# Decoder layer on one core: reordered projections and a batched block-inverse merge

## Chip, cores and metric

The kernel runs on one core of a Trainium2 chip. The metric is the device time of one execution in microseconds (us), and the figure that counts is the median of the runs of a kernel. The core has four compute engines with a queue of their own each: PE (TensorE: matrix products into PSUM; its weight loads are shown apart as PEld), DVE (VectorE), ACT (ScalarE) and POOL (GpSimd). SP (SyncE) issues most of the transfers, ACT the others. Each engine works through its queue in the order in which the program left it.

## What is computed

One layer of a hybrid decoder on x of 1024 tokens by 1024 features, in float32. Cut to what matters here:

```python
h = rmsnorm(x, attn_norm_w)
proj = h @ w_in                       # 1024 x 3592
qkv_la, z_la, b_la, a_la, q_d, k_d, v_d = split(proj)
# group 1: gated DeltaNet, 4 heads of 128
q_la, k_la, v_la = split(silu(causal_conv(qkv_la, conv_w)))
L   = where(strict, (k_beta @ k^T) * decay, 0);  A = L + I     # per chunk
u, w = solve_lower_triangular(A, [v*beta, k_beta*exp(g)])
o_la = recurrence over the chunks with state S (128 x 128 per head)
o_la = rmsnorm(o_la, la_norm_w) * silu(z_la)
# group 2: differential attention, 4 heads, two softmax maps of 64 columns each
p   = softmax(q0 k0^T + bias) - lam * softmax(q1 k1^T + bias)
o_d = rmsnorm(p @ v_d) * (1 - lam_init)
x = x + concat([o_la, o_d]) @ w_out
x = x + (silu(h2 @ gate) * (h2 @ up)) @ w_down                 # h2 = rmsnorm(x)
return rmsnorm(x, final_norm_w)
```

The reference solves chunks of 64 tokens; the kernel uses chunks of 128, 8 per head, 32 in all.

## The kernel before

Every large product is split into three: an operand is a high part (`_h`) and a low part (`_l`, the rest), and `mm3` issues high x high, high x low and low x high into the same PSUM tile (L144, L145, L146). A projection of 128 output columns over all 1024 tokens, called a dense here, is 2 halves x 8 blocks of the input features x 3, so 48 products of 128x128 by 512 into one `big` tile of PSUM (128x1024). There are two `big` tiles, and four of 128x512 (`sm` and `fl`, two each), which the function `sm()` hands out in turn. A dense needs its 128 columns of weights in SBUF (`w_raw`, loaded by SP), their high part (`w_h`, ACT, L151) and their low part (`w_l`, on DVE in one instruction, L153, or on POOL in two, L157; an argument chooses).

The stages around the change, in the order of time:

- Conv, K and Q of the four DeltaNet heads (`dense_T` and `conv_silu`: ACT L433 and L437, three times DVE L435), the sums of squares, and the products K K^T and K Q^T (L478, L479), from which `At` and `intra` are made on DVE (L482, L485).
- The inverse of the 32x32 blocks on the diagonals, on DVE alone: four transposes (L504), then 31 times a product (L509) and a subtraction (L511), each in need of the one ahead, then two transposes (L514, L515) that give `DcT` and `Dc`. Beside it PE computes the four Z projections (`dense_T` with POOL for the low part, `silu` on ACT, a write to DRAM) and the V projection of head 0.
- Merging the 32-blocks to the inverse of 128x128 (`TT`), head by head: DVE spreads `DcT` and `Dc` to 128 columns (L537), then two levels of `At` x columns (L544, copied out by ACT L547), the upper update (L551) and in level 0 the lower one (L557), in two halves of four chunks, each product 128x128 by 128 though only some of the columns are read (L560, L563, L566). That is 40 products per head, 160 in all. A float32 product stands in the trace as two entries of PE, so a group of four is shown as x8.
- Transposes of K (L575) and V (L625), V projections of heads 1 to 3, the recurrence over 8 chunks (L640 to L680), and beside and behind the recurrence the attention's query and key projections of heads 0 and 1 (`qk_dense`): ACT L596 scales a half out of PSUM, ACT L597 rounds it to the high part, POOL L598 subtracts, and ACT issues the writes of `qh`, `ql` and `ks` to DRAM.
- Attention. SP loads `aqh`, `aql` (L720), `ak` (L702), `bias` (L705) and `avd` (L727) of head 0 from DRAM, and the first score product is L904. The order from here on is written out by hand, with projections of heads 2 and 3 as filler.

A scheduler that places each instruction orders the queues of PE, DVE, ACT, POOL and SP ahead of the attention, so code order and queue order differ.

Of the kernel before, what the change touches and what calls it, by code (L numbers as in the profile page):

```python
# [68 lines left out]
def decoder_kernel(ctx: ExitStack, tc: tile.TileContext, a: dict, out: bass.AP):  # L69
# [425 lines left out]
    def bx(name):  # L495
        return op.tile([P, T], F32, name="av", bufs=4)
# [16 lines left out]
    Dc = bx("Dc").rearrange("p (h c) -> p h c", c=32)  # L513
    nc.vector.transpose(out=DcT.rearrange("p h c -> p c h"), in_=X)  # L514
    nc.vector.transpose(out=Dc.rearrange("p h s -> p s h"), in_=X.rearrange("p c s -> p s c"))  # L515
    for h in range(H):
        zps = dense_T(C_Z + h * P, nc.gpsimd)
        sz = cvt()
        nc.scalar.activation(out=sz, in_=zps, func=AF.Silu)
        nc.scalar.dma_start(out=sz_dr[h], in_=sz)  # L520

    vts = []

    def v_dense(h):
        vt = cvt()
        conv_silu(dense_T(C_V + h * P, nc.gpsimd), 8 + h, vt)
        vts.append(vt)

    v_dense(0)
    TT = [opt("avl") for h in range(H)]  # L530
    quad_b = quad.rearrange("p (o q c) -> p o q c", o=1, q=4).broadcast_to([P, 8, 4, 32])
    K = []
    for h in range(H):
        Df = bx("Df").rearrange("p (j c) -> p j c", c=P)
        for dst, src in ((TT[h], DcT), (Df, Dc)):
            sb = src[:, h * 8:h * 8 + 8, :].rearrange("p j (o c) -> p j o c", o=1).broadcast_to([P, 8, 4, 32])
            nc.vector.tensor_tensor(out=dst.rearrange("p j (q c) -> p j q c", q=4), in0=sb, in1=quad_b, op=ALU.mult)  # L537
        Z1 = bx("Z1").rearrange("p (j c) -> p j c", c=P)
        for level in range(2):
            for half in range(2):  # L540
                b0 = h * 8 + half * 4
                ps = sm()
                for jj in range(4):
                    nc.tensor.matmul(ps[:, jj * P:(jj + 1) * P], lhsT=At[:, b0 + jj, :], rhs=Df[:, half * 4 + jj, :],  # L544
                                     start=True, stop=True)
                zs = Z1[:, half * 4:half * 4 + 4, :]
                nc.scalar.copy(out=zs, in_=ps.rearrange("p (a b) -> p a b", a=4))  # L547
                ut = sm()
                utv = ut.rearrange("p (a b) -> p a b", a=4)
                for jj in range(4):  # L550
                    nc.tensor.matmul(ut[:, jj * P:(jj + 1) * P], lhsT=Z1[:, half * 4 + jj, :], rhs=TT[h][:, half * 4 + jj, :],  # L551
                                     start=True, stop=True)
                if level == 0:
                    un = sm()
                    unv = un.rearrange("p (a b) -> p a b", a=4)
                    for jj in range(4):
                        nc.tensor.matmul(un[:, jj * P:(jj + 1) * P], lhsT=TT[h][:, half * 4 + jj, :], rhs=Z1[:, half * 4 + jj, :],  # L557
                                         start=True, stop=True)
                    for r0 in (0, 64):
                        nc.vector.tensor_scalar(out=TT[h][r0:r0 + 32, half * 4:half * 4 + 4, r0 + 32:r0 + 64],  # L560
                                                in0=utv[r0:r0 + 32, :, r0 + 32:r0 + 64],
                                                scalar1=-1.0, scalar2=None, op0=ALU.mult)
                        nc.scalar.mul(out=Df[r0 + 32:r0 + 64, half * 4:half * 4 + 4, r0:r0 + 32],  # L563
                                      in_=unv[r0 + 32:r0 + 64, :, r0:r0 + 32], mul=-1.0)
                else:
                    nc.vector.tensor_scalar(out=TT[h][0:64, half * 4:half * 4 + 4, 64:128], in0=utv[0:64, :, 64:128],  # L566
                                            scalar1=-1.0, scalar2=None, op0=ALU.mult)
    Ktok = gp.tile([P, NHJ, P], F32, name="ak", bufs=1)
    for h in range(H):
        Kh = Ktok[:, h * 8:h * 8 + 8, :]  # L570
        for half in range(2):
            ps = sm()
            for jj in range(4):
                j = half * 4 + jj
                nc.tensor.transpose(ps[:, jj * P:(jj + 1) * P], KT[h][:, j * P:(j + 1) * P], ident)  # L575
            nc.scalar.copy(out=Kh[:, half * 4:half * 4 + 4, :], in_=ps.rearrange("p (a b) -> p a b", a=4))
        K.append(Kh)


    def qk_dense(h, is_q, ps_of, mid=None):  # L580
        if (h, is_q) not in raws:
            fetch((h, is_q), *qk_col(h, is_q))
        w = take((h, is_q), nc.gpsimd if h > 1 else None)
        yield 0
        sh = cvt(F32R)
        sl = cvt(F32R)
        for n in range(2):
            if n and mid:
                mid()
            ps = ps_of(n)  # L590
            wh, wl = w
            ns = slice(n * 512, (n + 1) * 512)
            for k in range(NK):
                mm3(ps, wh[:, k, :], wl[:, k, :], xT_h[:, k, ns], xT_l[:, k, ns], k == 0, k == NK - 1)
                yield 3
            nc.scalar.mul(out=sl[:, ns].bitcast(F32), in_=ps, mul=DH ** -0.5 if is_q else 1.0)  # L596
            nc.scalar.copy(out=sh[:, ns], in_=sl[:, ns].bitcast(F32))  # L597
            nc.gpsimd.tensor_tensor(out=sl[:, ns], in0=sl[:, ns].bitcast(F32), in1=sh[:, ns].bitcast(F32),  # L598
                                    op=ALU.subtract)
        if is_q:  # L600
            nc.scalar.dma_start(out=qh_dr[h], in_=sh.bitcast(F32))
# [9 lines left out]
    def run(gen):  # L611
        for _ in gen:
            pass

    Vn = [opt("av") for h in range(H)]
# [794 lines left out]
```

## Time and profile before

| | us |
|---|---|
| median of 3 runs | 1379.53 (1378.08 to 1379.64) |
| profiled execution | 1377.38 |
| its span in the trace | 1375.5 |
| PE busy | 1305.1 (95% of the span) |
| DVE busy | 768.1 (56%) |
| ACT busy | 497.1 (36%) |
| POOL busy | 262.5 (19%) |

The mean granted clock of TensorE over the span is 0.988 of full speed. An idle row of the timeline carries in brackets how long its engine stood before it and what released it. All moments below are us from the start of the span.

### The profile page before, as it was taken

How to read it: one execution, taken by the hardware profiler on the slowest of the kernel's cores; microseconds unless marked ns; L12 is line 12 of the kernel's file. 1: busy time of each engine (PE TensorE's matmuls, PEld its weight loads, DVE VectorE, ACT ScalarE, POOL GpSimd, SP SyncE). 2: the span in 40 equal slices, each digit the busy share in tenths (PEclk: the TensorE clock that was granted, in tenths of full speed). 3: DMA queues.
4: the chain of work that ended last, by engine and by line, in shares of the span. 5: the costliest groups of instructions: out<-in, count | busy, mean ns of one | idle time of the engine just before them, and what ended most of it. 6: DMA issues, size and time to landing. Idle time of an engine off the chain costs nothing.

```text
span 1375.5 us, 17042 instructions
## 1 busy us (share of the span) xinstructions
PE 1305.1 (95%) x6540; PEld 1086.2 (79%) x6540; DVE 768.1 (56%) x1282; ACT 497.1 (36%) x948; POOL 262.5 (19%) x211
## 2 busy tenths in 40 slices
PE   6999999899988998998889999999999999999997
PEld 6968888798967777887667877787878788788886
DVE  6516649625833675876884555455545536545325
ACT  5233321233733654553543333232323235112104
POOL 1010052100042331113332121211121214200003
PEclk9999999999998999999999999999999999999999
DMA  7321113101055655734432233222222248422003
GB/s 216 110 62 47 31 44 97 29 1 47 1 145 182 208 179 185 237 119 168 145 100 77 94 100 98 79 75 92 92 77 73 80 134 280 152 92 92 0 1 123
DMA packets 122425, 143.31 MB, mean 104 GB/s; under 512 B 13632, under 2 KB 90728, under 8 KB 122344
## 3 DMA queue, kind: packets, MB, share of 16 engines
q1 hardware_dynamic: 114432, 128.07, 30.0%
q10 hardware_dynamic: 7912, 14.16, 2.8%
q8 instruction: 51, 0.84, 0.3%
q14 instruction: 30, 0.25, 0.1%
HBM read 103.40 MB, written 38.80 MB: 103 GB/s over the span
## 4 chain that ended last, share of the span: by engine, by line
PE 70%; DVE 13%; DMA 5%; issue 4%; ACT 4%; POOL 3%; SPq 1%; POOLq 0%; DVEq 0%; ACTq 0%
PE big L1177 17%; PE sm L1177 8%; PE fl L144 4%; PE fl L145 4%; PE fl L146 4%; PE fl L1177 4%; PE big L144 3%; PE big L145 3%; PE big L146 3%; PE sm L144 3%; PE sm L146 3%; PE sm L145 3%; PE sm L961 1%; DVE tmp L509 1%; DMA ks<-cv 1%
## 5 line engine op out<-in xcount | busy, mean ns | idle before, releaser
L144 PE MATMUL big<-xT_h,w_h 128*128 128x512 f32 x320 | 127.8, 399 | 0.7 <-DVE cv L435 0.7
L146 PE MATMUL big<-xT_h,w_l 128*128 128x512 f32 x320 | 126.9, 397 | 0.5 <-DVE w_l L153 0.5
L145 PE MATMUL big<-xT_l,w_h 128*128 128x512 f32 x320 | 126.2, 394 | 0.0
L1190 DVE TENSOR_TENSOR av<-big,av 128x512 f32<-128x512 f32 x88 | 60.5, 689 | 109.3 <-PE big L1177 109.2
L157 POOL TENSOR_TENSOR w_l<-w_raw,w_h 128x512 fp32r<-128x512 f32 x36 | 49.0, 1384 | 244.0 <-ACT w_h L151 244.0
L1177 PE MATMUL big<-hT_h,cv 128*128 128x512 f32 x264 | 90.8, 405 | 2.4 <-DVE av L1190 2.4
L1177 PE MATMUL big<-hT_h,avl 128*128 128x512 f32 x264 | 89.2, 399 | 1.1 <-DVE av L1190 1.1
L151 ACT CAST w_h<-w_raw 128x1024 fp32r<-128x1024 f32 x32 | 33.5, 1051 | 110.5 <-PE big L145 94.7
L144 PEld LDWEIGHTS big<-xT_h,w_h 128*128 128x128 f32 x320 | 60.7, 190 | 13.9 <-issue 2.2
L146 PEld LDWEIGHTS big<-xT_h,w_l 128*128 128x128 f32 x320 | 60.5, 189 | 13.2 <-DVE w_l L153 0.9
L145 PEld LDWEIGHTS big<-xT_l,w_h 128*128 128x128 f32 x320 | 60.6, 189 | 12.1 <-issue 0.2
L1177 PEld LDWEIGHTS big<-hT_h,cv 128*128 128x128 f32 x264 | 50.4, 191 | 20.2 <-DVE av L1190 9.8
L1177 PEld LDWEIGHTS big<-hT_h,avl 128*128 128x128 f32 x264 | 49.5, 188 | 18.1 <-DVE av L1190 8.0
L1177 PE MATMUL sm<-hB_h,avl 128*128 128x512 f32 x176 | 58.8, 395 | 1.1 <-ACT hB_h L1107 1.1
L1082 POOL TENSOR_TENSOR avl<-xh,avl 128x512 fp32r<-128x512 f32 x23 | 30.8, 1338 | 148.2 <-ACT avl L1081 148.2
L1190 DVE TENSOR_TENSOR x<-fl,x 128x512 f32<-128x512 f32 x48 | 33.0, 687 | 45.6 <-PE fl L146 45.6
L1190 DVE TENSOR_TENSOR x<-sm,x 128x512 f32<-128x512 f32 x48 | 33.0, 687 | 44.8 <-PE sm L146 44.1
L1177 PE MATMUL sm<-hB_h,cv 128*128 128x512 f32 x176 | 57.9, 389 | 0.0
L919 ACT ACTIVATE ae<-big,mx 128x128 f32<-128x128 f32 (+7 forms) x64 | 47.3, 741 | 27.7 <-DVE mx L910 11.6
L1082 POOL TENSOR_TENSOR cv<-xh,cv 128x512 fp32r<-128x512 f32 x22 | 28.3, 1288 | 146.3 <-ACT cv L1081 146.3
L1145 DVE TENSOR_TENSOR xh<-w_raw 128x512 f32<-128x512 f32 x45 | 31.0, 689 | 45.1 <-DMA w_raw<-in_w_gate_up 45.1
L435 DVE SCALAR_TENSOR_TENSOR cv<-big,convw,cv 128x1023 f32<-128x1023 f32 (+2 forms) x36 | 46.0, 1278 | 15.0 <-ACT cv L433 14.4
(431 smaller groups left out, 3532.1 us busy)
## 6 DMA issues: line engine op xcount, KB each, us to landing
w_raw<-in_w_gate_up SPq DMA_DIRECT2D x44, 512.0 KB, 4.0
w_raw<-in_w_in SPq DMA_DIRECT2D x24, 512.0 KB, 4.0
act<-av SPq DMA_DIRECT2D x22, 512.0 KB, 2.6
w_raw<-act SPq DMA_DIRECT2D x22, 512.0 KB, 4.2
cv<-in_w_down SPq DMA_DIRECT2D x20, 512.0 KB, 4.4
xt<-in_x SPq DMA_DIRECT2D x8, 512.0 KB, 5.5
ks<-cv ACTq DMA_DIRECT2D x8, 512.0 KB, 12.5
aqh<-qh SPq DMA_DIRECT2D x16, 256.0 KB, 5.2
```

Source lines behind the costliest of these rows:

```text
L144: nc.tensor.matmul(ps, lhsT=lh, rhs=rh, start=start, stop=False)
L145: nc.tensor.matmul(ps, lhsT=lh, rhs=rl, start=False, stop=False)
L146: nc.tensor.matmul(ps, lhsT=ll, rhs=rh, start=False, stop=stop)
L151: nc.scalar.copy(out=h, in_=raw)
L157: eng.tensor_tensor(out=l[:, c], in0=raw[:, c], in1=h[:, c].bitcast(F32), op=ALU.subtract)
L435: nc.vector.scalar_tensor_tensor(out=acc[:, d:], in0=ps[:, :T - d], scalar=convw[:, ct, 3 - d:4 - d], in1=acc[:, d:], op0=ALU.mult, op1=AL ...
L509: nc.vector.tensor_tensor(out=tv, in0=B[:, i + 1:, i:i + 1].broadcast_to([P, nr, ncol]), in1=X[:, i:i + 1, :ncol].broadcast_to([P, nr, nco ...
L919: nc.scalar.activation(out=e[:, :n].rearrange("p (b c) -> p b c", b=nb), in_=s[:, :, :w], func=AF.Exp, bias=mx[:, m:m + 1], accum_out=zs[: ...
L1082: eng.tensor_tensor(out=l, in0=raw, in1=h.bitcast(F32), op=ALU.subtract)
L1145: nc.vector.tensor_tensor(out=r, in0=a0, in1=a1, op=alu)
L1177: nc.tensor.matmul(ps, lhsT=x[:, k, :], rhs=y[:, k, :], start=begin and k == 0 and n == 0, stop=k == HALF - 1 and n == 2, skip_group_check ...
L1190: nc.vector.tensor_tensor(out=out, in0=in0, in1=in1, op=ALU.add)
```

## The change

- The Z projections leave the place beside the inverse. They come behind the recurrence, with their low weight parts on DVE.
- The query and key projections of attention heads 0 and 1 (four `qk_dense`) take their place beside the inverse. For these two heads ACT writes the scaled half as the high part, and one DVE instruction (L536 of the new file) reads the same half from PSUM and gives the low part; POOL has no part in it.
- V of heads 0 and 1 are both computed ahead of the merging.
- The merging goes level by level over the four heads, with eight chunks in one PSUM tile. `sub_z` (L594) takes 64 columns of the moving operand, `un` (L606) 32, and both `ut` (L608, L621) have 64 columns in the stationary operand and 64 in the moving one. The number of products stays 160. The spreads (L583) write 64 columns of `Dc` in place of 128.

The diff, cut to its core (the lines of the new file are 21 to 23 higher from the attention on):

```diff
-    for h in range(H):
-        zps = dense_T(C_Z + h * P, nc.gpsimd)
-        ...
-    v_dense(0)
+    for h in range(2):
+        run(qk_dense(h, True, wide()))
+        run(qk_dense(h, False, wide()))
...
+    v_dense(0)
+    v_dense(1)
...
-            nc.scalar.mul(out=sl[:, ns].bitcast(F32), in_=ps, mul=DH ** -0.5 if is_q else 1.0)
+            scale = DH ** -0.5 if is_q else 1.0
+            if h < 2:
+                nc.scalar.mul(out=sh[:, ns], in_=ps, mul=scale)
+                nc.vector.scalar_tensor_tensor(out=sl[:, ns], in0=ps, scalar=scale, in1=sh[:, ns].bitcast(F32),
+                                               op0=ALU.mult, op1=ALU.subtract)
+                continue
+            nc.scalar.mul(out=sl[:, ns].bitcast(F32), in_=ps, mul=scale)
             nc.scalar.copy(out=sh[:, ns], in_=sl[:, ns].bitcast(F32))
             nc.gpsimd.tensor_tensor(out=sl[:, ns], in0=sl[:, ns].bitcast(F32), in1=sh[:, ns].bitcast(F32),
...
+    def sub_z(h):
+        ps = sm()
+        for j in range(NT):
+            nc.tensor.matmul(ps[:, j * 64:(j + 1) * 64], lhsT=At[:, h * 8 + j, :], rhs=cols[h][:, j, :],
+                             start=True, stop=True)
+        nc.scalar.copy(out=Z1[h], in_=ps.rearrange("p (j c) -> p j c", c=64))
...
+        for j in range(NT):
+            nc.tensor.matmul(un[:, j * 32:(j + 1) * 32], lhsT=TT[h][:, j, :], rhs=Z1[h][:, j, 0:32], start=True, stop=True)
+        for j in range(NT):
+            nc.tensor.matmul(ut[0:64, j * 64:(j + 1) * 64], lhsT=Z1[h][:, j, :], rhs=tth[:, j, :, 32:64],
+                             start=True, stop=True)
...
-        if h > 0:
+        if h > 1:
             v_dense(h)
...
-    for h in range(2):
-        run(qk_dense(h, True, wide()))
-        run(qk_dense(h, False, wide()))
+    for h in range(H):
+        zps = dense_T(C_Z + h * P, nc.vector)
+        sz = cvt()
+        nc.scalar.activation(out=sz, in_=zps, func=AF.Silu)
+        nc.scalar.dma_start(out=sz_dr[h], in_=sz)
```

On the queue of DVE at the start of the inverse there stood, before (`av` holds the blocks and their inverse, `ak` is `At`):

```order
L504 STREAM_TRANSPOSE av<-ak 32x1024 x4
L509 TENSOR_TENSOR tmp<-av 128x31
L511 TENSOR_TENSOR av<-av,tmp 128x31
L509 TENSOR_TENSOR tmp<-av 128x60
L511 TENSOR_TENSOR av<-av,tmp 128x30x2
L509 TENSOR_TENSOR tmp<-av 128x87
L511 TENSOR_TENSOR av<-av,tmp 128x29x3
```

and now, with `cv<-big,cv` the new evacuation of a query or key half:

```order
L504 STREAM_TRANSPOSE av<-ak 32x1024 x4
L536 SCALAR_TENSOR_TENSOR cv<-big,cv 128x512
L509 TENSOR_TENSOR tmp<-av 128x31
L153 TENSOR_TENSOR w_l<-w_raw,w_h 128x1024
L511 TENSOR_TENSOR av<-av,tmp 128x31
L509 TENSOR_TENSOR tmp<-av 128x60
L511 TENSOR_TENSOR av<-av,tmp 128x30x2
L509 TENSOR_TENSOR tmp<-av 128x87
```

Between the transposes and L514 there are now five L536 and two L153, one more L536 stands behind L515 and one behind the spreads. The eighth, of the first half, stands ahead of the transposes.

On the queue of PE at the same place, the change from the second dense of that stretch to the third read, before (`big_1805` and `big_1864` are Z of heads 1 and 2):

```order
L145 MATMUL big_1805<-xT_l_138,w_h_1800 128x512
L146 MATMUL big_1805<-xT_h_137,w_l_1801 128x512
L144 MATMUL big_1864<-xT_h_137,w_h_1859 128x512 [waits Activation_49]
L145 MATMUL big_1864<-xT_l_138,w_h_1859 128x512
L146 MATMUL big_1864<-xT_h_137,w_l_1860 128x512 [waits Pool_49]
L144 MATMUL big_1864<-xT_h_137,w_h_1859 128x512
```

and now (`big_1739` and `big_1802` are query and key of head 0, `big_1865` the query of head 1):

```order
L145 MATMUL big_1802<-xT_l_138,w_h_1805 128x512
L146 MATMUL big_1802<-xT_h_137,w_l_1806 128x512
L144 MATMUL big_1865<-xT_h_137,w_h_1868 128x512 [waits DVE_49]
L145 MATMUL big_1865<-xT_l_138,w_h_1868 128x512
L146 MATMUL big_1865<-xT_h_137,w_l_1869 128x512 [waits DVE_49]
L144 MATMUL big_1865<-xT_h_137,w_h_1868 128x512
L145 MATMUL big_1865<-xT_l_138,w_h_1868 128x512
L146 MATMUL big_1865<-xT_h_137,w_l_1869 128x512
L144 MATMUL big_1865<-xT_h_137,w_h_1868 128x512
L144 MATMUL big_1802<-xT_h_137,w_h_1805 128x512 [waits DVE_49]
```

The tile that `big_1865` takes is that of `big_1739`, and the wait is now for DVE's L536 on it, where it was for ACT alone.

On the queue of PE at the entry to the attention there stood, before (`big_3344` is the key projection of head 1, `fl_3457` the filler):

```order
L145 MATMUL big_3344<-xT_l_138,w_h_3347 128x512
L146 MATMUL big_3344<-xT_h_137,w_l_3348 128x512
L144 MATMUL fl_3457<-xT_h_137,w_h_3450 128x512 [waits Activation_49]
L904 MATMUL big_3433<-ak_3425,aqh_3419 128x128 [waits DMAHW5_49,DMAHW6_49,DMAHW1_49,Activation_49]
L905 MATMUL big_3433<-ak_3425,aql_3422 128x128 [waits DMAHW7_49,DMAHW0_49]
```

and now (`big_3293` is Z of head 3):

```order
L145 MATMUL big_3293<-xT_l_138,w_h_3289 128x512
L146 MATMUL big_3293<-xT_h_137,w_l_3290 128x512
L927 MATMUL big_3369<-ak_3361,aqh_3355 128x128 [waits DMAHW3_49,DMAHW7_49,DMAHW0_49,Activation_49]
L928 MATMUL big_3369<-ak_3361,aql_3358 128x128 [waits DMAHW2_49,DMAHW1_49]
```

The score product waits for the same loads as before, but what stands ahead of it on PE is Z, 128 of whose 192 products are still to come when the recurrence ends. SP still issues the loads of the weights of the head 2 projections ahead of `aqh`.

## Rows read from the trace of the kernel before

**Rows 1.** Windows of 10 us; columns as the first line says, PEclk the granted clock.

```profile
core 0: us, PE busy (x) PEld busy (x) DVE busy (x) ACT busy (x) POOL busy (x), PEclk, DMA share, GB/s
...
240.00:250.00 10.00, 6.08 (x27) 4.69 (x25) 9.52 (x18) 2.06 (x2) 2.94 (x2) 1.00 0.19 52
250.00:260.00 10.00, 8.32 (x42) 7.55 (x43) 9.93 (x9) 1.43 (x4) 0.55 (x1) 0.66 0.22 53
...
410.00:420.00 10.00, 2.76 (x9) 2.40 (x10) 0.57 (x2) 1.21 (x2) 1.26 (x1) 0.54 0.98 322
```

**Rows 2.** PE's timeline at the merging: start, duration, line, operation [idle before, releaser].

```profile
239.80 0.39 PE L144 MATMUL big<-xT_h,w_h 128*128 128x512 f32 x1
...
245.69 0.39 PE L146 MATMUL big<-xT_h,w_l 128*128 128x512 f32 x1
251.68 2.08 PE L544 MATMUL fl<-av,ak 128*128 128x128 f32 x8 [5.60 <-DVE av L537]
...
253.98 0.63 PE L145 MATMUL big<-xT_l,w_h 128*128 128x512 f32 x1
...
256.12 0.63 PE L144 MATMUL big<-xT_h,w_h 128*128 128x512 f32 x1
...
257.71 1.06 PE L557 MATMUL fl<-av,avl 128*128 128x128 f32 x8
258.60 1.06 PE L544 MATMUL sm<-av,ak 128*128 128x128 f32 x8
```

**Rows 3.** PE's timeline at the first score product.

```profile
417.24 0.45 PE L904 MATMUL big<-ak,aqh 128*128 128x128 f32 x1 [10.43 <-DMA ak<-ks]
...
418.66 0.63 PE L146 MATMUL fl<-xT_h,w_l 128*128 128x512 f32 x1
...
420.37 0.63 PE L144 MATMUL big<-xT_h,w_h 128*128 128x512 f32 x1
```

**Rows 4.** The chain that ended last, ahead of that product: start, duration, what.

```profile
392.87 1.83 POOL cv L598
...
394.73 13.25 DMA ks<-cv
...
408.04 9.11 DMA ak<-ks
```

**Rows 5.** DVE's timeline over the inverse.

```profile
207.67 8.13 DVE L504 STREAM_TRANSPOSE av<-ak 32x1024 f32<-32x1024 f32 x4
215.83 1.20 DVE L509 TENSOR_TENSOR tmp<-av 128x31 f32<-128x31 f32 x1
...
225.36 1.52 DVE L509 TENSOR_TENSOR tmp<-av 128x247 f32<-128x247 f32 x1
...
228.34 0.42 DVE L509 TENSOR_TENSOR tmp<-av 128x252 f32<-128x252 f32 x1
...
237.81 1.34 DVE L511 TENSOR_TENSOR av<-av,tmp 128x207 f32<-128x207 f32 x1
...
244.26 2.06 DVE L514 STREAM_TRANSPOSE av<-av 128x1024 f32<-128x1024 f32 x1
...
248.03 1.39 DVE L537 TENSOR_TENSOR avl<-av,mats 128x1024 f32<-128x1024 f32 x1
```

**Rows 6.** POOL's timeline, one of the four pairs of L157 beside the inverse.

```profile
225.31 2.72 POOL L157 TENSOR_TENSOR w_l<-w_raw,w_h 128x512 fp32r<-128x512 f32 x2 [8.33 <-ACT w_h L151]
```

**Rows 7.** Groups by line, 196 to 340 us: shapes, count, busy us, mean ns.

```profile
L153 DVE TENSOR_TENSOR w_l<-w_raw,w_h 128x1024 fp32r<-128x1024 f32 x2 | 2.5, 1225 | 7.4 <-ACT w_h L151 7.4
```

**Rows 8.** The page's costliest groups: count, busy us, mean ns, idle before.

```profile
L1190 DVE TENSOR_TENSOR av<-big,av 128x512 f32<-128x512 f32 x88 | 60.5, 689 | 109.3 <-PE big L1177 109.2
...
L144 PEld LDWEIGHTS big<-xT_h,w_h 128*128 128x128 f32 x320 | 60.7, 190 | 13.9 <-issue 2.2
```

**Rows 9.** The instructions of L279, durations in ns (min/median/max): a four-column stationary operand.

```profile
L279 PEld LDWEIGHTS fl<-rim,relb x2: 78/80/81, 71.5 to 71.5; 32*4 32x4 f32 x2
```

**Rows 10.** PE's timeline, a product with 32 moving columns (two entries).

```profile
81.62 0.39 PE L365 MATMUL sm<-g,mats 128*128 128x32 f32 x2
```

More of the change, by code (lines that the diff above doesn't have):

```diff
@@ L515, in decoder_kernel @@
     nc.vector.transpose(out=Dc.rearrange("p h s -> p s h"), in_=X.rearrange("p c s -> p s c"))
-    for h in range(H):
-        zps = dense_T(C_Z + h * P, nc.gpsimd)
[L518 to L527, printed above, removed]
-    v_dense(0)
-    TT = [opt("avl") for h in range(H)]
-    quad_b = quad.rearrange("p (o q c) -> p o q c", o=1, q=4).broadcast_to([P, 8, 4, 32])
@@ L532, in decoder_kernel @@
[L532 to L577, printed above, removed]
     def qk_dense(h, is_q, ps_of, mid=None):
@@ L613, in run, with v_dense, halves @@
             pass
+    for h in range(2):
+        run(qk_dense(h, True, wide()))
+        run(qk_dense(h, False, wide()))
+    vts = []
+    def v_dense(h):
+        vt = cvt()
+        conv_silu(dense_T(C_V + h * P, nc.gpsimd), 8 + h, vt)
+        vts.append(vt)
+    v_dense(0)
+    v_dense(1)
+    TT = [opt("avl") for h in range(H)]
+    K = []
+    def halves(name):
+        two = [bx(name).rearrange("p (h j c) -> p h j c", h=2, c=64) for _ in range(2)]
+        return [two[h // 2][:, h % 2] for h in range(H)]
@@ new lines, in spread @@
+    def spread(dst, src, q0, nq, step):
+        sb = src.rearrange("p j (o c) -> p j o c", o=1).broadcast_to([P, 8, nq, 32])
+        qb = quad.rearrange("p (o q c) -> p o q c", o=1, q=4)[:, :, q0:q0 + step * nq:step, :].broadcast_to([P, 8, nq, 32])
+        nc.vector.tensor_tensor(out=dst.rearrange("p j (q c) -> p j q c", c=32), in0=sb, in1=qb, op=ALU.mult)
+    cols = halves("cols")
+    for h in range(H):
+        spread(cols[h], Dc[:, h * 8:h * 8 + 8, :], 0, 2, 2)
+        spread(TT[h], DcT[:, h * 8:h * 8 + 8, :], 0, 4, 1)
@@ new lines, in decoder_kernel @@
+    Z1 = halves("Z1")
+    def sub_z(h):
[4 more added lines that the diff above has]
+        nc.scalar.copy(out=Z1[h], in_=ps.rearrange("p (j c) -> p j c", c=64))
+    for h in range(H):
+        sub_z(h)
+    for h in range(H):
+        spread(cols[h][:, :, 32:64], Dc[:, h * 8:h * 8 + 8, :], 1, 1, 1)
+    for h in range(H):
+        un, ut = sm(), sm()
+        tth = TT[h].rearrange("p j (a c) -> p j a c", c=64)
+        for j in range(NT):
[3 more added lines that the diff above has]
+                             start=True, stop=True)
+        nc.scalar.mul(out=cols[h][32:64, :, 0:32], in_=un[32:64, 0:256].rearrange("p (j c) -> p j c", c=32), mul=-1.0)
+        utv = ut.rearrange("p (j c) -> p j c", c=64)
+        for o in range(2):
+            nc.vector.tensor_scalar(out=TT[h][64 * o:64 * o + 32, :, 64 * o + 32:64 * o + 64],
+                                    in0=utv[32 * o:32 * o + 32, :, 32 * o:32 * o + 32],
+                                    scalar1=-1.0, scalar2=None, op0=ALU.mult)
@@ new lines, in decoder_kernel @@
+    for h in range(H):
+        sub_z(h)
+    for h in range(H):
+        ut = sm()
+        for j in range(NT):
+            nc.tensor.matmul(ut[0:64, j * 64:(j + 1) * 64], lhsT=Z1[h][:, j, :], rhs=TT[h][:, j, 64:128],
+                             start=True, stop=True)
+        nc.vector.tensor_scalar(out=TT[h][0:64, :, 64:128], in0=ut[0:64].rearrange("p (j c) -> p j c", c=64),
+                                scalar1=-1.0, scalar2=None, op0=ALU.mult)
+    Ktok = gp.tile([P, NHJ, P], F32, name="ak", bufs=1)
@@ L615, in decoder_kernel @@
+    for h in range(H):
+        Kh = Ktok[:, h * 8:h * 8 + 8, :]
+        for half in range(2):
+            ps = sm()
+            for jj in range(4):
+                j = half * 4 + jj
+                nc.tensor.transpose(ps[:, jj * P:(jj + 1) * P], KT[h][:, j * P:(j + 1) * P], ident)
+            nc.scalar.copy(out=Kh[:, half * 4:half * 4 + 4, :], in_=ps.rearrange("p (a b) -> p a b", a=4))
+        K.append(Kh)
     Vn = [opt("av") for h in range(H)]
@@ L686, in decoder_kernel @@
     nc.vector.tensor_tensor(out=oms, in0=oms, in1=rq, op=ALU.mult)
-    for h in range(2):
-        run(qk_dense(h, True, wide()))
-        run(qk_dense(h, False, wide()))
+    for h in range(H):
+        zps = dense_T(C_Z + h * P, nc.vector)
+        sz = cvt()
+        nc.scalar.activation(out=sz, in_=zps, func=AF.Silu)
+        nc.scalar.dma_start(out=sz_dr[h], in_=sz)
     close_gp()
```

## The prediction

> **What bounds the kernel now.** I read the windows first. PE is busy nearly everywhere, so a gain has to come from its idle places or from fewer passes. In the stretch that the change touches there are two such places, 240 to 260 and 400 to 420 us, and in both the granted clock drops as well, to 0.66 and 0.54 in one window [rows 1].
>
> PE's timeline gives them in detail. At the merging PE stands 5.60 us for DVE's L537, the spread that follows the inverse [rows 2]. Then it runs at half speed for a while: the group of eight entries at 251.68 takes 2.08 us where the same at 258.60 takes 1.06, and five dense products from 253.98 to 256.12 are 0.428 apart, where 26 steps from 239.80 to 245.69 are 0.2265 apart [rows 2]. The two are the 1.2 and 2.4 GHz levels. Seven products at this pitch cost 7 x 0.2 = 1.4 and the group 1.0, so the place costs 5.6 + 2.4 = 8.0 us.
>
> At the first score product PE stands 10.43 us for `ak` [rows 3]. The chain says why: the write of `ks` took 13.25 us behind POOL's subtraction, and the load of `ak` 9.11 behind that [rows 4]. Four products from 418.66 to 420.37 are again 0.4275 apart [rows 3]; six at that pitch cost 1.2, the score products about 0.3, so the place costs 11.9 us.
>
> DVE's timeline shows what the first place waits for: transposes of 8.13 us, then a chain from 215.83 to 244.26 in which nothing is idle, then 3.8 us to the first spread at 248.03 [rows 5].
>
> **The second idle place.** `qh`, `ql` and `ks` of head 0 are now written more than 100 us ahead of their loads, so the 13.25 us leaves the path. The 9.11 us of `ak` stay, and on SP the loads of the head 2 weights still stand ahead. These need the buffers that Z's last two splits free. Behind the recurrence PE has 128 products of Z, 128 x 0.2265 = 29.0 us. The split of Z's last weights can be done some 10 us into that (32 products of the second Z, then the cast and an L153 of 1.2 [rows 7]), the loads ahead of `ak` take some 5 us, and 9.11 more gives 24 of 29. So all of it is hidden, with 5 us to spare: minus 11.9. At worst it all comes back.
>
> **The first idle place goes, and a wait in the middle takes its seat.** A dense half of Q or K is now evacuated by ACT and then by DVE's L536, which stands in the queue of the inverse. `big` has two tiles, so the third dense can't start before L536 on the first is done, and that stands behind the transposes. Before, the 208 products from the last of K K^T to the gap end at 245.9, so they began at 245.9 - 208 x 0.2265 = 198.8 [rows 2]. Now PE gets 43 products done and stands at 208.5. The transposes end at 215.8 [rows 5], L536 is a 128x512 DVE instruction with an operand in PSUM as L1190 is, 0.69 us [rows 8]: PE goes on at 216.5, having stood 8.0 us.
>
> From there the chain of DVE sets the pace, since L536 of the first half of the fourth dense stands behind L515 and the second half of that tile waits for it. The chain took 28.4 us from 215.83 to 244.26 [rows 5]. In it four instructions from 225.36 to 237.81 took 1.3 to 1.5 in place of 0.42, and the first 1.2 [rows 5], each time beside a pair of POOL's subtractions [rows 6]: some 4.9 us that go with Z. V's two pairs, moved forward, can put back 2 us each. Four L536 and two L153 (1.225 [rows 7]) are added to the chain: 4 x 0.69 + 2 x 1.225 = 5.2. So L515's successor starts at 216.5 + 28.4 - 4.9 + 5.2 + 3.8 = 249.0 without V's pairs, and at 253.9 with nothing gained from POOL; with the last L536 of 0.7 that is 249.7 to 254.6, and I take 252, the middle, since the pairs' places are not fixed by the order. Behind it are 24 + 27 + 48 = 99 products of Q/K and V, 22.4 us: V of head 1 ends at 274.4. Without a wait, the 259 products would end at 198.8 + 58.7 = 257.5. The waits cost 16.9 us (14.6 to 19.5), and what the clock loses behind the 8 us stands inside that, because DVE's chain is the later one. Three products fewer stand ahead of the sums of squares than Z had there: 0.7 more. In exchange the 8.0 of the old place are gone, since the spreads are done long before 274.
>
> **The merging.** 160 products are 320 entries at (258.60 - 257.71) / 8 = 0.111 us [rows 2], 35.6 us before, and as many after. Fewer moving columns bring nothing: two entries with 32 columns take 0.39 [rows 10], an entry alone about 0.28 (1.06 less seven steps), so they too are 0.11 apart. 64 stationary columns, in 128 of the entries, stand in no row. A load of 128 columns takes 190 ns [rows 8], one of 4 columns 80 [rows 9], 0.89 ns per column; 64 columns fewer would be 57 ns fewer and 64 moving columns are half the stream, so 0.111 could become 0.055. The bounds are 0 and 7.1 us of gain; I take 7.1, because the row with four columns says that the load does follow the columns.
>
> The Trainium skill has the same as a rule: "TensorE: Matmul & The Clock Gate", section "LDWEIGHTS (loading the stationary operand)", puts the load at the number of columns over 1.2, in ns, whatever the rows. By it, as an estimate, the 128 entries would save 6.9 us. If rows were what counts, as the change keeps all 128 of them, they would save nothing, and the time would be that of the rival on the columns below.
>
> **At nothing.** Z's casts, `silu` and L153 beside the recurrence replace those of Q and K, which had L153 on DVE there too; the 64-column spreads and V's convolutions have the 20 us up to 274 as cover on DVE, and would cost their 1.3 us each without it; POOL loses the L598 of two heads, which only `ks` waited for. The order behind the first score product is the same.
>
> **The sum.** 16.9 + 0.7 - 8.0 - 7.1 - 11.9 = -9.4, so 1368.0 against the profiled execution of 1377.38. That execution lies 2.15 under the median of 1379.53, so in terms of the median it is 1370.1.
>
> **Rivals.** *Only the transposes make PE wait.* If POOL's pairs cost the chain nothing and the later L536 come in time, PE loses 8.0 and some 2.4 of clock in place of 16.9: 1363.6. For it speaks that the chain loses 4.9 us; against it, that the last L536 stands behind L515 wherever PE is.
>
> *64 columns cost what 128 cost.* Then 7.1 comes back: 1377.2. For it, that no row shows an entry under 0.11; against it, the four-column load.
>
> *The loads are late.* SP takes its issues in order; should the head 2 weights wait for the last Z split to be later than I think, `ak` lands behind Z's end, and each us costs one, up to the whole 11.9: 1376 to 1382.
>
> *Lockstep, on the slower side.* DVE's L536 waits in its queue for PE's half and ACT's copy, and the chain of the inverse with it; PE then waits for the next L536. If both wait in turn, a half costs PE's 24 products, 5.4, plus a copy and L536, 1.3, plus a sixth of the chain, 4.6: 11.3 in place of 5.4, and six halves 35 in place of 16.9: 1388. It decides when the waits cost more than 16.9 + 9.4 + 2.8 = 29 us, that is, when L536 behind L515 ends after 264. Against it: by the counts PE reaches each half 0 to 3 us ahead of DVE, so DVE hardly waits.
>
> **How the numbers follow.** The measurement of this kernel tells about 0.2%, 2.8 us, from no change. Forecast 0.52 (1364 to 1376), transposes only 0.13, columns 0.17, loads 0.08, lockstep 0.10. Faster: 0.50 + 0.13 + 0.08 + 0.03 = 0.74; within 0.2%: 0.17; slower: 0.09. The range 1362 to 1378 leaves out lockstep, late loads and the far end of the first rival.
>
> **What would show it.** Right: an idle row of about 8 us on PE near 208 with DVE as releaser and a low clock behind it; V of head 1 done near 274; no idle at L594; L608 and L621 in half the time per entry of L606; the first score product right behind Z. Wrong: L536 behind L515 before 249 or after 255; L608 at 0.11; a bracket with `ak` at L927; DVE idle rows that PE or ACT ends between L509 and L511.

## Result and the profile after

The changed kernel takes 1364.51 us (median of 4 runs, 1363.61 to 1370.49) against 1378.8 for the kernel before on the same chip. The ratio is 0.99 with a 95% interval of 0.9875 to 0.9925, so it is faster by some 14 us, about 1%. The profiled execution took 1363.61 with a span of 1361.5; before, these were 1377.38 and 1375.5. The prediction was 1370.1 with a range of 1362 to 1378.

The first view is the list of waits of PE between 180 and 420 us: what waited, for whom, the total in us, how often, and the longest.

```profile
PE big L144 <- DVE cv L536: 10.0, 4, 6.3
PE big L144 <- ACT cv L535: 0.7, 1, 0.7
```

This is all that the view lists there. The 5.60 at the merging [rows 2] and the 10.43 at the first score product [rows 3] are gone. In their place PE stands four times for DVE's new evacuation L536. PE's timeline (start, duration, line, operation, in brackets the idle time before and its releaser) shows these four, and the products behind the first of them:

```profile
214.47 0.79 PE L144 MATMUL big<-xT_h,w_h 128*128 128x512 f32 x1 [6.28 <-DVE cv L536]
...
216.31 0.63 PE L144 MATMUL big<-xT_h,w_h 128*128 128x512 f32 x1
216.74 0.63 PE L145 MATMUL big<-xT_l,w_h 128*128 128x512 f32 x1
...
218.48 0.80 PE L144 MATMUL big<-xT_h,w_h 128*128 128x512 f32 x1 [0.26 <-DVE cv L536]
...
241.21 0.50 PE L144 MATMUL big<-xT_h,w_h 128*128 128x512 f32 x1 [1.74 <-DVE cv L536]
...
248.00 0.50 PE L144 MATMUL big<-xT_h,w_h 128*128 128x512 f32 x1 [1.74 <-DVE cv L536]
```

Behind the 6.28 two products are 0.43 apart, twice the full pitch. The 1.2 GHz level now stands here. The windows of 10 us (columns as in [rows 1]) show where it went and where it stayed away:

```profile
210.00:220.00 10.00, 5.24 (x12) 3.29 (x13) 9.58 (x19) 0.60 (x1) 0.00 (x0) 0.66 0.34 105
...
240.00:250.00 10.00, 7.06 (x30) 5.53 (x31) 9.69 (x17) 0.60 (x1) 0.40 (x1) 1.00 0.42 130
...
280.00:290.00 10.00, 10.00 (x98) 9.13 (x95) 2.49 (x6) 2.88 (x5) 0.00 (x0) 1.00 0.01 2
...
400.00:410.00 10.00, 10.00 (x48) 8.36 (x47) 0.35 (x1) 1.09 (x3) 1.82 (x2) 1.00 1.04 323
```

The merging and the start of the attention run without a gap and at 1.00. DVE's timeline shows what the first wait hung on, and that the chain of the inverse now carries other work:

```profile
203.46 0.18 DVE L491 TENSOR_SCALAR rqs<-rqs 128x32 f32<-128x32 f32 x1 [5.82 <-POOL rqs L490]
...
205.99 7.71 DVE L504 STREAM_TRANSPOSE av<-ak 32x1024 f32<-32x1024 f32 x4
213.73 0.69 DVE L536 SCALAR_TENSOR_TENSOR cv<-big,cv 128x512 fp32r<-128x512 f32 x1
...
237.62 0.32 DVE L509 TENSOR_TENSOR tmp<-av 128x156 f32<-128x156 f32 x1
237.98 1.29 DVE L511 TENSOR_TENSOR av<-av,tmp 128x156 f32<-128x156 f32 x1
239.31 1.25 DVE L509 TENSOR_TENSOR tmp<-av 128x135 f32<-128x135 f32 x1
...
247.28 0.67 DVE L536 SCALAR_TENSOR_TENSOR cv<-big,cv 128x512 fp32r<-128x512 f32 x1
```

Two of the chain's steps take 1.29 and 1.25 where their neighbour of the same size takes 0.32. They are beside this pair on POOL, the only one in the chain:

```profile
237.69 2.70 POOL L157 TENSOR_TENSOR w_l<-w_raw,w_h 128x512 fp32r<-128x512 f32 x2 [34.26 <-ACT w_h L151]
```

The merging, again PE's timeline. A row is 16 entries, so the start of the next row less its own, over 16, is the pitch:

```profile
270.57 1.89 PE L594 MATMUL fl<-av,ak 128*128 128x64 f32 x16
272.30 1.95 PE L594 MATMUL sm<-av,ak 128*128 128x64 f32 x16
274.09 1.95 PE L594 MATMUL fl<-av,ak 128*128 128x64 f32 x16
...
279.52 1.15 PE L608 MATMUL sm<-avl,av 128*64 128x64 f32 x16
280.59 1.97 PE L606 MATMUL fl<-av,avl 128*128 128x32 f32 x16
...
299.73 1.10 PE L621 MATMUL sm<-avl,av 128*64 128x64 f32 x16
300.66 1.10 PE L621 MATMUL fl<-avl,av 128*64 128x64 f32 x16
```

With 128 stationary columns it is 1.79 / 16 = 0.112 us (L594 at 272.30), with 64 it is 0.93 / 16 = 0.058 in L621 and 1.07 / 16 = 0.067 in L608. The weight loads by groups (count, busy us, mean ns, idle before) are shorter by 54 ns with the narrow operand:

```profile
L594 PEld LDWEIGHTS fl<-av,ak 128*128 128x128 f32 x64 | 7.5, 192 | 0.1
...
L608 PEld LDWEIGHTS sm<-avl,av 128*64 128x64 f32 x64 | 4.0, 138 | 0.5 <-issue 0.4
...
L632 PEld LDWEIGHTS fl<-ident,KT 128*128 128x128 f32 x16 | 1.8, 141 | 0.1
```

But the third row, transpositions with 128 columns, has 141 too: the length of a load in such a row is not its columns alone, and the pitch is the surer reading.

Last, PE at the first score product, and SP's issue of `ak`, which landed 8.2 us later:

```profile
409.00 0.22 PE L927 MATMUL big<-ak,aqh 128*128 128x128 f32 x1
```

```profile
396.64 0.59 SPq L725 DMA_DIRECT2D ak<-ks  x1
```

`ak` is there at about 404.9, and Z ends at 409.0: no bracket, with 4 us to spare.

**Where the time went, by landmarks.** Two rows of PE from the kernel before, the first transposition of K (the end of the merging) and the score step that is 256 columns wide, then the same two from the changed kernel:

```profile
299.21 0.60 PE L575 MATMUL fl<-ident,KT 128*128 128x128 f32 x4
...
430.22 0.28 PE L904 MATMUL big<-ak,aqh 128*128 128x256 f32 x1
```

```profile
302.62 0.66 PE L632 MATMUL fl<-ident,KT 128*128 128x128 f32 x4
...
414.90 0.28 PE L927 MATMUL big<-ak,aqh 128*128 128x256 f32 x1
```

The end of the merging is at 302.62, was 299.21: later by 3.41, but with 21 more dense products done (4.8 us), so at equal work it is earlier by 1.4. The score step starts at 414.90, was 430.22: between the two landmarks 18.7 are gained, less those 4.8, so 13.9. The end of the span is 14.0 earlier, not 15.3: some 1.3 are given back behind that step. There the waits of the score lines for ACT's exponentials grew from 5.8 to 6.7, but other waits shrank by as much (31.0 in all before, 30.8 now), so where the 1.3 went is not shown.

### The profile page after: what moved, and what is told of

It is laid out like the page before. It is cut to its first block, busy times and chain, and to the rows that moved or that the text cites. A ratio compares the mean times of both kernels' runs of the same rounds, so it can differ in the third digit from the quotient of the medians.

```text
span 1361.5 us, 16980 instructions
## 1 busy us (share of the span) xinstructions
PE 1298.3 (95%) x6540; PEld 1078.0 (79%) x6540; DVE 766.1 (56%) x1286; ACT 484.7 (36%) x920; POOL 240.6 (18%) x195
## 4 chain that ended last, share of the span: by engine, by line
PE 72%; DVE 12%; DMA 5%; issue 4%; ACT 4%; POOL 2%; SPq 1%; POOLq 0%; DVEq 0%; ACTq 0%
PE big L1200 17%; PE sm L1200 8%; PE big L144 4%; PE big L146 4%; PE big L145 4%; PE fl L144 4%; PE fl L146 4%; PE fl L145 4%; PE fl L1200 4%; PE sm L144 3%; PE sm L145 3%; PE sm L146 3%; PE sm L984 1%; DVE tmp L509 1%; DVE av L511 1%
## 5 line engine op out<-in xcount | busy, mean ns | idle before, releaser
L144 PE MATMUL big<-xT_h,w_h 128*128 128x512 f32 x320 | 128.2, 401 | 10.7 <-DVE cv L536 10.0
L157 POOL TENSOR_TENSOR w_l<-w_raw,w_h 128x512 fp32r<-128x512 f32 x28 | 37.8, 1371 | 124.5 <-ACT w_h L151 123.3
L1105 POOL TENSOR_TENSOR cv<-xh,cv 128x512 fp32r<-128x512 f32 x22 | 28.4, 1289 | 146.7 <-ACT cv L1104 146.7
L1200 PE MATMUL big<-hT_l,cv 128*128 128x512 f32 x132 | 52.6, 398 | 0.0
## 6 DMA issues: line engine op xcount, KB each, us to landing
ks<-cv ACTq DMA_DIRECT2D x8, 512.0 KB, 13.7
```

Of the source, the lines that this page charges most:

```text
L144: nc.tensor.matmul(ps, lhsT=lh, rhs=rh, start=start, stop=False)
L157: eng.tensor_tensor(out=l[:, c], in0=raw[:, c], in1=h[:, c].bitcast(F32), op=ALU.subtract)
L1105: eng.tensor_tensor(out=l, in0=raw, in1=h.bitcast(F32), op=ALU.subtract)
L1200: nc.tensor.matmul(ps, lhsT=x[:, k, :], rhs=y[:, k, :], start=begin and k == 0 and n == 0, stop=k == HALF - 1 and n == 2, skip_group_check ...
```

## Experiments

The theory after the result: the waits of PE for DVE's L536, hung on the transposes and on the inverse's chain, cost about 13 us. The two old idle places and the 64-column weights more than pay for them. Rivals: that the waits cost little because the inverse sets the time in any case; that the loads of head 0 alone make the gain; and that 64 stationary columns bring nothing.

**The weights' columns.** The same products as in the changed kernel, but in `ut` 128 stationary columns in place of 64 (in 7 of 8 chunks; the other 64 are not read).

```diff
-            nc.tensor.matmul(ut[0:64, j * 64:(j + 1) * 64], lhsT=Z1[h][:, j, :], ...
+            wide_z = Z1[h].rearrange("p j c -> p (j c)")[:, j * 64:min(j * 64 + 128, 512)]
+            nc.tensor.matmul(ut[0:wide_z.shape[1], j * 64:(j + 1) * 64], lhsT=wide_z, ...
```

> The changed kernel, with a stationary operand of 128 columns in place of 64 in seven of eight products of the two ut updates (the added columns are the next chunk's; their results are not read). 112 of the 256 entries that the two lines L594 and L606 leave beside them are touched. If the load of the weights sets the pitch of these products and PE is the pace of the merging, they go from some 0.06 us apart back to 0.11 and the kernel loses 5 to 6 us against the changed one (1369 to 1371). If the merging is paced by ACT, DVE or the wait between levels, the time stays within 1.5 us of the changed one.

The merging has 320 entries in all and 128 in the two `ut` lines; the 256 of this text and the 448 of the one on 64 columns below are miscounts, on which no figure rests. The run took 1393.89 (ratio to before 1.0111, 1.0086 to 1.0136): 29 us more than the changed kernel, five times the 5 to 6 that the columns should cost. A window of it, then two of its PE rows:

```profile
300.00:310.00 10.00, 10.00 (x48) 9.77 (x48) 0.83 (x2) 0.94 (x2) 0.00 (x0) 0.50 0.00 0
```

```profile
290.67 1.93 PE L609 MATMUL sm<-avl,av 128*128 128x64 f32 x16
...
298.90 3.63 PE L609 MATMUL sm<-avl,av 128*128 128x64 f32 x16
```

The granted clock falls to 0.50, the 1.2 GHz level, while PE is busy without a gap, and stays there from 300 to 330. The same 16 entries take 1.93 at one level and 3.63 at the other. So this run doesn't price the columns; it shows a second effect. The next two runs were made to take that away: they give `un` 64 moving columns in place of 32 (32 of them not read): one on top of the wide weights, the other on the changed kernel alone.

```diff
-            nc.tensor.matmul(un[:, j * 32:(j + 1) * 32], lhsT=TT[h][:, j, :], rhs=Z1[h][:, j, 0:32], ...
+            nc.tensor.matmul(un[:, j * 64:(j + 1) * 64], lhsT=TT[h][:, j, :], rhs=Z1[h][:, j, :], ...
```

> The kernel with 128 stationary columns in the ut updates (1393.9, low clock through the merging) and 64 moving columns in place of 32 in L606, whose added columns are not read. If the low granted clock there comes from products that stream few columns while each waits for its load of 128, 64 of the 448 entries now stream twice as much at the same pitch, and the clock falls later, for less time, or not at all: at least 5 us less than 1393.9. If the clock falls for another reason, the time stays at 1392 to 1396 or rises with the added columns.

> The changed kernel with 64 moving columns in place of 32 in L606, the added ones not read. At 0.11 us per entry for the load of 128 columns the added ones cost nothing: 1363 to 1365, as the changed kernel. If columns set the pitch, 64 entries cost 0.05 more each, 3 us. If the changed kernel loses time to the clock in some runs, fewer of these do.

With wide weights it took 1371.71 (0.9957, 0.9944 to 0.9969), and the clock stays high:

```profile
300.00:310.00 10.00, 10.00 (x87) 9.60 (x86) 2.05 (x3) 1.62 (x3) 0.00 (x0) 1.00 0.01 2
```

The same work plus 32 idle columns in 64 entries is 22 us faster, and the clock is all of it: the six windows from 280 to 340 of the slow kernel (0.68, 0.84, three times 0.50, 0.76) lack 22.2 us of full clock (10 x (1 - PEclk), summed), those of the fast one none. On the changed kernel the 64 columns bring nothing: 1365.38 (0.9907, 0.9892 to 0.9921), against 1365.12 (0.9906, 0.9889 to 0.9922) for the changed kernel itself, measured beside it.

> The changed kernel once more, for the spread of its runs beside those of the others on this chip: most at 1364, and some 4 to 7 us higher where the granted clock falls within the merging, as the mean clock of each run should show (0.985 against 0.989).

The difference of the two with 64 moving columns, 1371.71 - 1365.38 = 6.3 us, is the price of the 128 stationary columns with the clock held, over 112 entries 0.056 each. In the two traces the merging itself is 38.0 and 31.2 us long, 6.8 apart, behind the same 10.7 us of waits. The rows give the same: 0.12 us apart with 128 columns, 0.058 to 0.067 with 64.

**The two parts alone.** First everything but the swap: new merging, V of both heads ahead, but Z beside the inverse with POOL's splits, Q and K behind the recurrence with the old evacuation.

```diff
-            if h < 2:
+            if h < 0:
...
-    for h in range(2):
-        run(qk_dense(h, True, wide()))
-        run(qk_dense(h, False, wide()))
+    for h in range(H):
+        zps = dense_T(C_Z + h * P, nc.gpsimd)
...
-    for h in range(H):
-        zps = dense_T(C_Z + h * P, nc.vector)
...
+    for h in range(2):
+        run(qk_dense(h, True, wide()))
+        run(qk_dense(h, False, wide()))
```

> The changed merging and both V ahead of it, but Z stays beside the inverse and Q and K behind the recurrence, evacuated as before. If my sums hold, the place at the merging closes (8.0 us) since V of head 1 covers the spreads, the narrow weights bring 6, the wait for ak stays: 1364 to 1366, the same as the whole change. If the swap of Z with Q and K is what carries the gain, the time stays above 1371.

Then the swap alone: the kernel before, with Q and K beside the inverse, DVE's evacuation, Z behind the recurrence, and the old merging with V of head 0 alone ahead of it.

```diff
-    for h in range(H):
-        zps = dense_T(C_Z + h * P, nc.gpsimd)
-        ...
+    for h in range(2):
+        run(qk_dense(h, True, wide()))
+        run(qk_dense(h, False, wide()))
...
+            if h < 2:
+                nc.scalar.mul(out=sh[:, ns], in_=ps, mul=scale)
+                nc.vector.scalar_tensor_tensor(out=sl[:, ns], in0=ps, scalar=scale, in1=sh[:, ns].bitcast(F32), ...
+                continue
```

> The kernel before with Z and Q/K swapped and the new DVE evacuation, the merging and V of head 1 as they were. By my sums the wait for ak and its cold clock go (12 to 13 us), the old place at the merging closes behind the new waits (8 us), and the waits for L536 cost 13.7: 1371 to 1373. If the waits for L536 are covered by something else, or if the old place stays open besides, it is 1364 or less, or 1379 and more.

The first took 1365.97 (0.9904, 0.9879 to 0.9929), the second 1372.2 (0.9961, 0.9947 to 0.9974); the kernel before, measured beside them, took 1378.15. Their waits of PE, 180 to 420, the first kernel's and then the second's:

```profile
PE big L927 <- DMA ak<-ks: 10.1, 1, 10.1
PE big L144 <- DVE cv L435: 0.7, 1, 0.7
PE big L146 <- DVE w_l L153: 0.5, 1, 0.5
```

```profile
PE big L144 <- DVE cv L535: 10.0, 4, 6.3
PE big L144 <- ACT cv L534: 0.7, 1, 0.7
```

Alone, the merging and V bring 12 us and the swap 6; together 14 in place of 18. Without the swap PE stands 10.1 for `ak`, with it 10.0 for L536. On top of the other part the swap has bought about 1 us (1365.97 against 1364.51 and 1365.12, the two measurements of the changed kernel), which these runs can't tell from nothing: one wait paid for the other. The profiled execution of the first was 1369.71, its other runs 1365.6 to 1366.2. Its merging has the groups of the changed kernel in the same order, but at a low clock in part:

```profile
260.00:270.00 10.00, 10.00 (x76) 9.84 (x75) 5.61 (x8) 3.66 (x6) 2.50 (x2) 0.74 0.22 52
270.00:280.00 10.00, 10.00 (x73) 8.60 (x72) 1.66 (x4) 2.88 (x5) 0.00 (x0) 0.75 0.01 2
```

**The wait on DVE.** If L536 is what holds PE, its work on POOL should give most of the 13 us back. ACT, ACT, POOL as before the change:

```diff
-            if h < 2:
+            if h < 0:
```

> The changed kernel, with the low part of the Q and K halves made as before (ACT scales, ACT rounds, POOL subtracts) and not by DVE out of PSUM. If the waits of 10.0 us for L536 and the low clock behind them come only from DVE's queue holding the PSUM tiles, V of head 1 ends near 258 in place of 270.6 and the time falls by 9 to 12 us, to 1352 to 1356, though POOL now slows some links of the inverse. If the DVE chain is late for the merging all the same (POOL's eight subtractions, each costing a link about 1 us), the wait moves to the first merging product and the gain is under 4 us.

It took 1363.32 (0.9885, 0.9853 to 0.9917), like the changed kernel, and its merging starts at 270.66 where that of the changed kernel starts at 270.57. PE's timeline:

```profile
218.92 0.80 PE L146 MATMUL big<-xT_h,w_l 128*128 128x512 f32 x1 [7.57 <-DVE w_l L153]
```

The wait went to the next instruction behind the transposes: L153, the low part of the weights. The theory of L536 was too narrow. PE waits for whatever stands on DVE behind the transposes and the chain. So the next runs move the weights' low parts to POOL as well, for the third dense alone (`take` is the function whose argument says which engine), once with 32 and once with 64 columns in `un`:

```diff
-        w = take((h, is_q), nc.gpsimd if h > 1 else None)
+        w = take((h, is_q), nc.gpsimd if h > 1 or (h, is_q) == (1, True) else None)
```

> The changed kernel with the Q and K halves' low parts on POOL, and of the weights only those of the second query on POOL (the ones PE stood 7.6 us for); the other three stay on DVE. If both what PE waits for and what POOL takes from the inverse count, V of head 1 ends near 259, the spreads are done 3 to 4 us earlier than with all splits on POOL, so ACT's silu of V of head 0 no longer holds up the copies of the merging for 5 us: 1352 to 1358. If the merging is entered before DVE is ready all the same, PE waits there, the clock falls in the narrow products, and the time is 1360 to 1366.

> The kernel before this one in the list, with 64 moving columns in place of 32 in L606, the added ones not read. If the low clock in the merging is what the narrow products bring once PE has waited there, it is shorter and the time 3 to 6 us lower; if the clock stays high in both, the times agree within 1.5 us.

1365.83 (0.9904, 0.9887 to 0.9922) and 1365.32 (0.9899, 0.9881 to 0.9917), and in both the wait is one dense further on and longer (the row is the first one's):

```profile
230.74 0.80 PE L146 MATMUL big<-xT_h,w_l 128*128 128x512 f32 x1 [10.14 <-DVE w_l L153]
```

The granted clock in the merging was high in both, so the columns of `un` made no difference here. With POOL for the low parts of all four weights:

```diff
-        w = take((h, is_q), nc.gpsimd if h > 1 else None)
+        w = take((h, is_q), nc.gpsimd)
```

> The changed kernel with the low parts of the Q and K halves on POOL as before the change, and the low parts of their weights on POOL too (two L157 in place of one L153), so that no product of Q or K waits for DVE. If DVE's queue behind the transposes is all that holds PE there (it held L536, and with L536 gone L153 for 7.6 us), V of head 1 ends near 258 in place of 270.6 and the time falls to 1350 to 1355. If POOL's subtractions slow the inverse enough for the spreads to be late, PE waits at the first merging product instead and the time stays above 1358.

1364.16 (0.9896, 0.9876 to 0.9916). PE does not wait for DVE in Q and K any more (1.3 us for ACT are left), and the merging starts at 260.65 in place of 270.57. So the inverse does not hold the changed kernel to 270: that rival falls. But inside the merging PE stands again:

```profile
260.65 1.89 PE L594 MATMUL fl<-av,ak 128*128 128x64 f32 x16
...
272.97 3.62 PE L606 MATMUL fl<-av,avl 128*128 128x32 f32 x16 [5.07 <-ACT av L596]
```

ACT's timeline, and the row of DVE that ends just ahead of L437:

```profile
269.44 1.06 ACT L437 ACTIVATE cv<-cv 128x1024 f32<-128x1024 f32 x1 [17.63 <-issue]
...
272.35 0.57 ACT L596 COPY av<-fl 128x512 f32<-128x512 f32 x1
```

```profile
265.44 3.92 DVE L435 SCALAR_TENSOR_TENSOR cv<-big,convw,cv 128x1023 f32<-128x1023 f32 x3
```

The copy that PE waits for stands on ACT behind L437, the `silu` of V of head 0. That needs V's convolution (L435), which DVE has queued behind the inverse and the spreads and ends at 269.36; the view names no releaser for the 17.63, so this is read from the order and the times. The row of L606 is also at half speed (3.62 for 16 entries). Ten us were won and given back at two places, and both have a remedy: V's convolution and `silu` behind the merging's first copies (a one-column copy from `Z1` ties them in the queues), and 64 columns in `un`. The next kernel has both, with all splits on POOL as here; the diff shows the first:

```diff
-    v_dense(0)
-    v_dense(1)
+    v_ps = [dense_T(C_V + h * P, nc.gpsimd) for h in range(2)]
...
         sub_z(h)
+    for h in range(2):
+        vt = cvt()
+        nc.scalar.copy(out=vt[:, 0:1], in_=Z1[2 + h][:, 0, 0:1])
+        conv_silu(v_ps[h], 8 + h, vt)
+        vts.append(vt)
```

> All splits of Q and K on POOL (as in the kernel that stood 5.1 us at L606), 64 moving columns in L606, and the silu of V of heads 0 and 1 tied behind the copies of the first merging level by a one-column copy on ACT, so that the copies no longer queue behind DVE's convolution. If the gain that is lost sits only in that queue and in the low clock behind it, PE enters the merging at 260 and runs through it: 1350 to 1356. If the clock falls in the narrow products without an idle ahead of them (there are no dense products between them any more), or DVE's convolutions hold up the updates, the time is 1358 to 1364.

1355.05 (1353.52 to 1356.87; ratio 0.984, 0.9824 to 0.9857): 23 us under the kernel before and 10 under the changed one. Its waits of PE between 180 and 420, then two windows of its merging:

```profile
PE big L144 <- ACT cv L539: 1.3, 3, 0.7
PE sm L593 <- DVE av L582: 0.6, 1, 0.6
```

```profile
270.00:280.00 10.00, 10.00 (x101) 9.73 (x101) 9.63 (x12) 2.65 (x6) 0.00 (x0) 1.00 0.01 2
280.00:290.00 10.00, 10.00 (x92) 8.98 (x92) 1.51 (x3) 3.45 (x6) 0.00 (x0) 1.00 0.01 2
```

Ten us of waits have become 1.9, the merging starts 11.4 us earlier, and some 10 us of the 13 that the waits cost have come back. Last, this kernel with 32 columns in `un` again, all else equal:

> The fastest kernel so far (1355.05) with the 32 moving columns of the change put back in L606 and nothing else changed; 64 entries stream half as much at the same pitch. If used columns alone are what takes the clock down in the merging, the granted clock falls there and the time rises by 4 us or more. If the fall needs an idle of PE ahead of it, or more entries that wait for 128 columns, the time stays within 1.5 us.

1365.44 (0.9907, 0.9879 to 0.9935), 10 us slower. The waits are the same 0.6 at the merging; the windows are not:

```profile
270.00:280.00 10.00, 10.00 (x73) 9.70 (x72) 8.72 (x10) 1.78 (x4) 0.00 (x0) 0.56 0.01 2
280.00:290.00 10.00, 10.00 (x62) 9.88 (x62) 0.91 (x3) 2.15 (x5) 0.00 (x0) 0.61 0.00 0
```

The four windows from 260 to 300 lack 10.2 us of full clock. The profiled execution is the fastest of the four runs (1360.63 to 1368.71), 7 us over that of the kernel with 64 columns. So taking the waits away was not enough by itself: with 32 columns the tied `silu` brought nothing that the runs can tell (1364.16 without it, 1365.44 with it). What 64 columns would bring without the tie was not run.

## Why the prediction was right, and where its sizes were off

The forecast held in direction and mechanism; 1364.5 lies 5.6 under the predicted 1370.1 and near the low end of the range, because the two terms that were off most, the wait in the middle and the second place, were off to the same side. By its steps:

- *The wait takes a seat in the middle.* Right: PE stands for DVE's L536 behind the transposes, the clock falls behind it, and L536 behind L515 holds the last half. The size was 16.9; the measured one is 13.6, from V of head 1 ending at 270.57, against the 257.0 that 259 products at full pitch would give from a start half a us earlier than assumed. 10.0 of that are the four idle rows, the rest the low clock and the 0.7 for ACT. L536 behind L515 ended at 247.95 and not at 252, and three inputs make up the 4. The chain began at 214.34 and not at 216.5, mostly because L491 takes 0.18 where it took 1.26 (Z's subtractions on POOL no longer stand beside it) and the transposes 7.71 for 8.13. The four L536 and two L153 made the chain 3.9 longer and not 5.2: each starts some 0.08 ahead of the end of the instruction before it (L536 at 217.74 behind an L509 from 217.52 that takes 0.30), where the steps of the chain start some 0.03 behind it. And one pair of POOL's subtractions fell into it, for 1.9, where the middle of the range stands for 2.4. What was left of the chain, 23.4 without POOL and the added work, is what the prediction took (28.4 - 4.9). The prediction had named "before 249" as a sign that it is wrong: the theory of the chain stands, the assumed time did not.
- *What POOL's pairs do to the chain.* Seen at 237.98: 1.29 for a step of 0.32. The Trainium skill, "SBUF — State Buffer", section "Who interferes with whom", says that VectorE and GpSimd share one pair of SBUF ports under an exclusive lock. These rows agree in that the steps beside the pair are later, by about 1 us for each of two; the lock itself they do not show.
- *64 stationary columns.* Right in kind: 0.058 to 0.067 per entry in place of 0.112. The gain read from the rows is 6.2, predicted was 7.1; the first level's entries did not reach 0.055. The pair of runs gives 6.3 for 112 of the 128 entries, 7.2 for all, and its intervals are too wide, some 2 us to either side of each run, to tell the two apart. The rival that the columns cost alike is refuted. The Trainium skill, "TensorE: Matmul & The Clock Gate", section "LDWEIGHTS (loading the stationary operand)", with its columns over 1.2, gives an estimate of 53 ns less for 64 columns fewer (6.8 us over the 128 entries, where the prediction wrote 6.9), and these loads differ by 192 - 138 = 54; the 141 of L632, with 128 columns, does not fit it, so the pitch and the pair of runs carry this point, not the loads.
- *The old place at the merging.* Right: nothing idle at L594, since the last spread is done at 254.9.
- *The second place.* Right in mechanism, `ak` landing 4 us before Z ends (5 predicted). The term was 11.9; the stretch gained 13.9. The waits of 0.7 and 0.5 that PE had there for DVE's convolution and L153 went too; some 0.8 were not traced.
- *Lockstep* did not appear, nor did the loads come late. *Transposes only* gave a time near the measured one, 1363.6, but for another reason: the later L536 did hold PE, 1.74 twice.

The measured terms, with the 8.0 of the old place as read from the rows before, give 13.6 - 8.0 - 6.2 - 13.9 = -14.5; less 0.5 for the earlier start and plus 1.3 given back behind the score step that is -13.7, and the spans differ by 14.0. The 0.7 for three products fewer ahead could not be seen apart from the rest. The prediction's "at nothing" part held, but for these 1.3 at most.

Left open: why the clock stays at 1.00 in the changed kernel's own merging, though the kernel without the swap has the same narrow products in the same order and fell. Also whether the 1370.49 among its runs, at a mean clock of 0.985 where the others have 0.989 to 0.990, was such a fall; only its mean clock is known.

## What to carry to other kernels

An evacuation or a weight split put on an engine that runs a long serial chain waits for that chain, and so does the engine that needs the buffer. Look for the whole queue, not for the one instruction: taken off DVE, the wait went from L536 to L153, then a dense further on, then to a `silu` in front of a copy on ACT. And look at the granted clock when the waits are gone: the time moved only in the kernel that held it too, 1355.05 with 64 columns in `un` against 1365.44 with 32. Two changes that each remove an idle place need not add up, when one pays with a new wait of the same length.

## What the runs showed of the hardware beyond this

**Fewer columns can cost more.** In a stretch where PE is busy without a gap, the granted clock fell from the 2.4 to the 1.2 GHz level when the products were narrow: 0.50 from 300 to 330 us with 32 moving columns in `un` and 128 stationary ones in `ut`, 0.56 and 0.61 in the fastest kernel with 32 columns. In the first of these the clock rose behind the eight dense products from 287.37 (16 entries take 1.93 at 290.67) and fell again among the narrow ones (3.63 at 298.90). Each time 64 columns in `un` restored 1.00, without any time of their own: `un`'s entries are 0.11 to 0.12 us apart either way. That was worth 22 us in one pair and 10 in the other. In each pair the waits ahead of the fall are alike with 32 and 64 columns (10.7 us in the first, about 2 in the second), so idle time does not tell the two apart. The scheduler also placed some dense products anew (8 became 4 within the merging in the first pair, 10 became 8 in the second), but behind the start of the fall. In two other pairs (the changed kernel, and the one with the wait of 10.14) the columns made no difference; in both the clock stayed up with 32 columns as well. Both have 10 us of waiting for DVE ahead of the merging, and the kernel without the swap, which has no such wait there, fell with the same products (0.74 and 0.75). But the kernel with 128 stationary columns in `ut` and 32 moving ones in `un` fell behind the same 10 us. So long waits ahead do not keep the clock up in general, and what does is not shown.

**64 columns in the weights halve the pitch of narrow float32 products**, 0.112 to 0.058, which fewer moving columns did not.
